# A hybrid decoder layer in one core: late tiles two abreast, the last gate pair swapped, stores and loads moved to GpSimd's queue, the scan tied behind the level

## The chip, the core and the metric

The kernel runs on one core of one Trainium2 chip. The core has five engines that run their own instruction streams in order: TensorE (PE, with the weight loads shown apart as PEld), VectorE (DVE), ScalarE (ACT), GpSimd (POOL) and SyncE (SP). A DMA is issued by one of the engines' queues and moves data between the chip's memory and the core's SBUF; matmuls write to PSUM. The metric is the device time of one execution in microseconds. Times are medians of several runs; durations of single instructions come from one profiled execution.

## The reference

One layer on a sequence of 1024 steps, 1024 wide, in float32. `h` is an RMS norm of `x`. One input projection of `h` gives the inputs of two branches and two gates. Branch A is an RWKV-7 time mix: 8 heads of 64, each a 64x64 state with a decay and a rank-one correction in every step. Branch B is S5, a diagonal complex state space with a GELU and a gated linear unit (GLU) behind it. Both are projected, gated and added, go through an output projection and a post norm, and are added to `x`. Then a gated MLP with a causal convolution of width 3 follows, with norms on both sides.

```python
h = rms_norm(x, norm_mix_pre[l])
proj = h @ w_in[l]
gates = jax.nn.sigmoid(proj[..., N_RWKV_COLS + S5_WIDTH:] + b_gate[l])
g_rwkv, g_s5 = jnp.split(gates, 2, axis=-1)
o_rwkv = rwkv7_branch(p_rwkv, ...) @ w_branch_rwkv[l]
o_s5 = s5_branch(u_s5, ...) @ w_branch_s5[l]
mixed = (g_rwkv * o_rwkv + g_s5 * o_s5) @ w_out[l]
x = x + rms_norm(mixed, norm_mix_post[l])
h = rms_norm(x, norm_ffn_pre[l])
f = conv_ffn(h, ffn_w_up[l], ffn_conv_w[l], ffn_conv_b[l], ffn_w_down[l])
x = x + rms_norm(f, norm_ffn_post[l])
```

## The kernel before

**Tiles.** Everything is held transposed: channels on the 128 partitions, time along the row, in two halves `th` of 512 steps. A product in float32 is made of three matmuls with reduced operands: each operand is split into a high part (a cast on ACT) and a low part (a subtraction on VectorE), and high x high, high x low and low x high are added up in PSUM. `mm3_steps` (L163) issues the three matmuls of each of the input blocks `k`; `load_w` (L145) loads a weight tile on SP's queue and splits it (L157 on ACT, L158 on VectorE). `split` and `split_half` (L226, L230) do it for activations. The two halves of `h` lie in the tile pools `hp[0]` and `hp[1]`, as pairs `hh0..7` and `hl0..7`, and those places are used again for later pairs.

**Order.** TensorE runs in the order in which the program is written (`manual_schedule`). The other engines' order is made by a scheduler that takes instructions by priority as its own model finds them ready; it is fixed before the run. The program text itself is woven from generators ("lanes") by `drive` (L186): a lane yields how long its matmuls take and how long to wait before its next piece, on a planner's clock `now`; in the gaps the `fill` list runs (`background`, L210), which holds the large projections. The constants `T_...` at L1905 to L1913 are such waiting times.

**Stages to about 960 us.** The norm and S5's inputs come first. Then the fill runs through the rest of the input projection (`mix_in`, L1009) and the 16 gate tiles (`gate_tiles`, L1030), of which the last two go as one pair through `inproj` (L915): both for `th` 0, then `merge_values`, then both for `th` 1. Their results go through the buffers `ev` (4 of them early, 3 later) to scratch tensors in memory: `RKV`, `TZ`, `TA`, `TG` (L999, L1006) and `GT` (L1035), with DMAs on SP.

Beside the fill the RWKV branch runs in four batches (2 groups of heads x 2 halves). `rwkv_front` (L642) loads `k`, `tz`, `ta`, `r` and later `v` (L659, SP) into the ring `ld` of 10 tiles, scans the decays (L674, VectorE), takes exponentials, makes products on GpSimd (L683, L684) and then the small matrices (L704, L706). `rwkv_inv` (L750) solves small triangular systems on VectorE (L763, L765), with GpSimd's DMAs before and after (L712, L756, L768, L775). `rwkv_level` (L777) transposes on VectorE (L787) and multiplies (L790, L792). `rwkv_chain` (L805) goes through 8 steps in series. `rwkv_out` (L866) normalizes and stores the branch's output `YR` (L911); the last batch keeps its output on the core, and its `bv` and `TG` loads (L878) go over GpSimd.

**The merge.** `merge` (L1159) forms the gated sum for `th` 0: eight gate tiles on branch A, S5's inputs loaded, put through GELU and split after the first of them, four GLU tiles (`glu_tile`, L1128) and eight gate tiles on branch B. `out_glu` (L1219) makes the output projection for `th` 0, with at most one GLU tile of `th` 1 after each of the tiles 3 to 7. `merge_s5` and `merge_rk` (L1228, L1246) form the sum for `th` 1, and `outproj(1)` (L1309) its output projection. `mid_norms` (L1313) is the post norm and the next norm; for `th` 0 it starts as soon as its sums `y0` are there, beside `merge_rk`. `first_units` (L1390) begins the MLP with the normalized `th` 0, which is split in the order 0, 4, 1, 5, 2, 6, 3, 7 and used in the order 0 to 7. The rest of the MLP (`fast_up`, `down`) isn't touched.

Of the kernel before, what the change touches and what calls it, by code (L numbers as in the profile page):

```python
# [72 lines left out]
class Kern:  # L73
# [89 lines left out]
    def mm3_steps(self, ps, w, wk, xh, xl):  # L163

        wh, wl = w
        n = len(xh)
        for k in range(n):
            j = wk + k
            self.open += (k == 0) - (k == n - 1)
# [3 lines left out]
            mm(ps, a, xh[k], start=k == 0, stop=False)  # L173
            mm(ps, a, xl[k], start=False, stop=False)  # L174
            mm(ps, b, xh[k], start=False, stop=k == n - 1)  # L175
            yield 0.68

# [464 lines left out]
    def rwkv_front(self, d, u):  # L642
# [14 lines left out]
        def ld(src):  # L657
            t = self.tg("ld", NLD)
            nc.sync.dma_start(t, src[:, o])  # L659
# [14 lines left out]
        V.tensor_tensor_scan(tz, self.cst("smask"), tz, 0.0, ALU.mult, ALU.add)  # L674
# [7 lines left out]
        for h, sl in enumerate(HS):  # L682
            G.tensor_tensor(ar1[h], c64(r)[sl], pe[sl, :, 1:65], ALU.mult)  # L683
            G.tensor_tensor(bk1[h], c64(tk)[sl], c64(tz)[sl], ALU.mult)  # L684
# [92 lines left out]
    def rwkv_level(self, d):  # L777
# [8 lines left out]
        for h, sl in enumerate(top):  # L786
            V.transpose(xz[sl].rearrange("p u c t -> p (u c) t"), gr[sl, :, :, h, sl].rearrange("p u c t -> p (u c) t"))  # L787
# [77 lines left out]

    def rwkv_out(self, d):  # L866
# [29 lines left out]
        yield 0, T_LN  # L896
        for u in range(2):
# [12 lines left out]
            else:  # L910
                nc.sync.dma_start(self.YR[p][:, o], y1)  # L911
# [3 lines left out]
    def inproj(self, *jobs, between=None):  # L915

        ws = [self.load_w(self.a["w_in"][mt]) for mt, _ in jobs]
        for th in range(2):
# [4 lines left out]
            if between and th == 0:  # L923
# [204 lines left out]
    def glu_tile(self, m, xs, t, y, to):  # L1128

        nc = self.nc  # L1130
        w = self.load_w(self.a["w_glu"][m])
        ps = self.gmp()
# [15 lines left out]
    def merge_values(self):  # L1148

        if self.outs < 2:  # L1150
            return
        self.br0 = []
        for k in range(4):
            y = self.tg("ld", NLD)
            self.nc.gpsimd.dma_start(y, self.YR[k][:, 0:512])
            self.br0.append(self.pair(0, k))
            self.split(*self.br0[k], y)

    def merge(self, mg):  # L1159
# [6 lines left out]
        br = self.br0  # L1166
        xs = []

        def inputs():
            for b in range(4):  # L1170
# [825 lines left out]
```

## Time and profile before

| | |
|---|---|
| median of 3 runs | 1628.59 us (1625.99 to 1630.82) |
| the profiled execution | 1626.5 us, its span 1624.7 us |
| mean granted TensorE clock | 0.967 |
| busy: TensorE, VectorE, ACT, GpSimd | 1505.0, 1157.2, 717.6, 175.9 us |

The span runs from the first instruction to the last. A busy digit of the page stands for a fortieth of the span, 40.6 us, in tenths. A granted clock of 0.5 means that matmuls take twice as long. A row of the timeline has the start, the duration, the engine, the line of the kernel, the operation and its tiles, and in brackets how long the engine stood idle before it and what ended that. A row of the groups has, behind the count, the busy time in us, the mean of one in ns, and the idle time before them with its releasers. A row of the waits has who waited for what, the us in total, how often, and the longest.

### The profile page before, as it was taken

How to read it: one execution, taken by the hardware profiler on the slowest of the kernel's cores; microseconds unless marked ns; L12 is line 12 of the kernel's file. 1: busy time of each engine (PE TensorE's matmuls, PEld its weight loads, DVE VectorE, ACT ScalarE, POOL GpSimd, SP SyncE). 2: the span in 40 equal slices, each digit the busy share in tenths (PEclk: the TensorE clock that was granted, in tenths of full speed). 3: DMA queues.
4: the chain of work that ended last, by engine and by line, in shares of the span. 5: the costliest groups of instructions: out<-in, count | busy, mean ns of one | idle time of the engine just before them, and what ended most of it. 6: DMA issues, size and time to landing. Idle time of an engine off the chain costs nothing. (4 is left out here: it accounts for less than half of the span.)

```text
span 1624.7 us, 23434 instructions
## 1 busy us (share of the span) xinstructions
PE 1505.0 (93%) x8644; PEld 1200.3 (74%) x8644; DVE 1157.2 (71%) x2103; ACT 717.6 (44%) x1173; POOL 175.9 (11%) x251
## 2 busy tenths in 40 slices
PE   5998998999989997899978999999999999999995
PEld 4887887787666774666756878788888888788784
DVE  7888774565534687575478479987777777788777
ACT  5445433232444344446633445544454444443451
POOL 0030003133012133211020000000000000000000
PEclk9999999999998997999988999999999999999997
DMA  5353344343341256535255363322222224862722
GB/s 190 110 158 124 97 130 143 117 130 116 90 145 67 76 179 175 142 106 163 84 187 190 107 193 130 137 71 91 78 78 91 91 79 160 293 227 96 234 85 104
DMA packets 116387, 213.72 MB, mean 132 GB/s; under 512 B 22272, under 2 KB 28416, under 8 KB 116272
## 3 DMA queue, kind: packets, MB, share of 16 engines
q1 hardware_dynamic: 102960, 175.78, 33.8%
q0 software_dynamic: 11152, 32.20, 6.7%
q10 hardware_dynamic: 2160, 4.24, 0.7%
q8 instruction: 68, 1.11, 0.3%
q14 instruction: 47, 0.39, 0.1%
HBM read 157.12 MB, written 52.95 MB: 129 GB/s over the span
## 5 line engine op out<-in xcount | busy, mean ns | idle before, releaser
L173 PE MATMUL gm<-hh,wh 128*128 128x512 f32 x688 | 298.5, 434 | 17.9 <-DVE ev L961 5.5
L174 PE MATMUL gm<-hl,wh 128*128 128x512 f32 x688 | 277.8, 404 | 3.3 <-DVE hl L1126 2.0
L175 PE MATMUL gm<-hh,wl 128*128 128x512 f32 x688 | 276.4, 402 | 0.0
L158 DVE TENSOR_TENSOR wl<-wf,wh 128x512 fp32r<-128x512 f32 x183 | 127.9, 700 | 115.1 <-ACT wh L157 113.4
L157 ACT CAST wh<-wf 128x512 fp32r<-128x512 f32 x183 | 113.3, 620 | 185.2 <-PE gm L174 94.0
L173 PEld LDWEIGHTS gm<-hh,wh 128*128 128x128 f32 x688 | 133.5, 194 | 54.6 <-ACT hh L1125 6.3
L174 PEld LDWEIGHTS gm<-hl,wh 128*128 128x128 f32 x688 | 134.0, 195 | 30.6 <-DVE hl L228 4.3
L175 PEld LDWEIGHTS gm<-hh,wl 128*128 128x128 f32 x688 | 133.6, 194 | 30.2 <-DVE wl L158 0.7
L1608 PE MATMUL d<-xl,wh 128*128 128x512 f32 x308 | 120.3, 391 | 3.1 <-DVE xl L228 3.1
L1607 PE MATMUL d<-xh,wh 128*128 128x512 f32 x308 | 120.2, 390 | 2.0 <-DVE zg L1463 2.0
L1609 PE MATMUL d<-xh,wl 128*128 128x512 f32 x308 | 119.9, 389 | 0.0
L1433 PE MATMUL rp<-t,h 128*128 128x512 f32 x216 | 84.4, 391 | 2.2 <-ACT p L1447 1.6
L1435 PE MATMUL rp<-t,l 128*128 128x512 f32 x216 | 84.2, 390 | 0.5 <-DVE l L228 0.5
L1434 PE MATMUL rp<-t,h 128*128 128x512 f32 x216 | 84.1, 389 | 0.0
L1608 PEld LDWEIGHTS d<-xl,wh 128*128 128x128 f32 x308 | 57.8, 188 | 16.7 <-DVE xl L228 4.8
L1607 PEld LDWEIGHTS d<-xh,wh 128*128 128x128 f32 x308 | 57.8, 188 | 14.4 <-DVE zg L1463 2.4
L1609 PEld LDWEIGHTS d<-xh,wl 128*128 128x128 f32 x308 | 57.8, 188 | 11.9
L227 ACT CAST h<-r 128x1024 fp32r<-128x1024 f32 x34 | 35.8, 1054 | 61.1 <-PE rp L1434 29.6
L228 DVE TENSOR_TENSOR l<-r,h 128x1024 fp32r<-128x1024 f32 x34 | 41.6, 1225 | 29.2 <-ACT h L227 27.7
L1454 DVE SCALAR_TENSOR_TENSOR y<-zv,vecs,y 128x1023 f32<-128x1023 f32 (+1 forms) x36 | 46.1, 1281 | 8.6 <-ACT y L1452 8.6
L1433 PEld LDWEIGHTS rp<-t,h 128*128 128x128 f32 x216 | 40.5, 188 | 11.8 <-ACT p L1447 2.4
L1447 ACT COPY p<-rp 128x512 f32<-128x512 f32 x54 | 31.1, 575 | 37.2 <-PE rp L1435 37.2
(446 smaller groups left out, 3400.4 us busy)
## 6 DMA issues: line engine op xcount, KB each, us to landing
wf<-in_w_in_dram SPq DMA_DIRECT2D x72, 256.0 KB, 3.0
r<-in_w_up_dram SPq DMA_DIRECT2D x36, 512.0 KB, 3.9
st<-in_w_down_dram SPq DMA_DIRECT2D x55, 256.0 KB, 4.3
st<-ACT SPq DMA_DIRECT2D x44, 256.0 KB, 4.7
wf<-in_w_up_dram SPq DMA_DIRECT2D x36, 256.0 KB, 2.9
ACT<-y POOLq DMA_DIRECT2D x18, 512.0 KB, 2.9
GT<-ev SPq DMA_DIRECT2D x32, 256.0 KB, 2.4
wf<-in_w_br_dram SPq DMA_DIRECT2D x32, 256.0 KB, 2.8
```

The costliest lines, as they stand in the source:

```text
L157: nc.scalar.copy(h[:, :n], f[:, :n])
L158: nc.vector.tensor_tensor(l[:, :n], f[:, :n], h[:, :n].bitcast(F32), ALU.subtract)
L173: mm(ps, a, xh[k], start=k == 0, stop=False)
L174: mm(ps, a, xl[k], start=False, stop=False)
L175: mm(ps, b, xh[k], start=False, stop=k == n - 1)
L1433: mm(ps, wh[:, c], xh, start=first and k == 0, stop=False, skip_group_check=True)
L1434: mm(ps, wh[:, c], xl, start=False, stop=False, skip_group_check=True)
L1435: mm(ps, wl[:, c], xh, start=False, stop=k == 3, skip_group_check=True)
L1454: V.scalar_tensor_tensor(y[:, lag:], z[:, 0:1024 - lag], self.vec(nme, i), y[:, lag:], ALU.mult, ALU.add)
L1607: mm(ps, wh[:, c], xh[:, x], start=start, stop=False, skip_group_check=True)
L1608: mm(ps, wh[:, c], xl[:, x], start=False, stop=False, skip_group_check=True)
L1609: mm(ps, wl[:, c], xh[:, x], start=False, stop=stop, skip_group_check=True)
```

## The change

It does nine things.

1. The stores of `RKV`, `TZ`, `TA`, `TG` and `GT`, the loads of `rwkv_front` and the loads and stores of `rwkv_out` are issued by GpSimd, not by SP.
2. The four products L683 and L684 of a front go from GpSimd to VectorE.
3. The scan L674 is ordered behind the transposes L787 of the level that was last written before it.
4. The pair of the last gate tiles runs `th` 1 first, then `th` 0. In between, `merge_values` now also loads and splits S5's inputs of `th` 0, into `hp[1]`; branch A's values go into `hp[1]` too, loaded straight into the tile of their low part, and the gate results of `merge` into `hp[0]`.
5. `out_glu` takes up to two GLU tiles after each of the tiles 4 to 7, and the GLU of `th` 1 fetches its factor `y` before its matmuls.
6. The last `rwkv_out` runs at a higher priority, and its planner wait is 11, not 16.
7. `mid_norms(0)` waits for the end of `merge_rk` and then 8, not 4; its wait before the sums is 24, not 55.
8. The first two tiles of `outproj(1)` run two abreast: inputs 0 to 5 of the first, 0 to 5 of the second, then 6 and 7 of both.
9. So does the first pair of `first_units`, in the order in which its inputs are split.

```diff
-    def mm3_steps(self, ps, w, wk, xh, xl):
+    def mm3_steps(self, ps, w, wk, xh, xl, ks=None, first=True, last=True):
...
+    def skewed(self, tiles, xs, ks, late):
+        xh, xl = [x[0] for x in xs], [x[1] for x in xs]
+        ps = [self.gmp() for _ in tiles]
+        ks = list(ks)
+        for p, (w, _) in zip(ps, tiles):
+            yield from self.mm3_steps(p, w, 0, xh, xl, ks[:-late], last=False)
+        for p, (w, use) in zip(ps, tiles):
+            yield from self.mm3_steps(p, w, 0, xh, xl, ks[-late:], first=False)
+            use(p)
...
-            nc.sync.dma_start(t, src[:, o])
+            G.dma_start(t, src[:, o])
...
-        V.tensor_tensor_scan(tz, self.cst("smask"), tz, 0.0, ALU.mult, ALU.add)
+        scan = V.tensor_tensor_scan(tz, self.cst("smask"), tz, 0.0, ALU.mult, ALU.add)
+        if self.levelled is not None:
+            self.tc.add_manual_dep(scan.ins, self.levelled.ins.name, ORDER)
...
-            G.tensor_tensor(ar1[h], c64(r)[sl], pe[sl, :, 1:65], ALU.mult)
-            G.tensor_tensor(bk1[h], c64(tk)[sl], c64(tz)[sl], ALU.mult)
+            V.tensor_tensor(ar1[h], c64(r)[sl], pe[sl, :, 1:65], ALU.mult)
+            V.tensor_tensor(bk1[h], c64(tk)[sl], c64(tz)[sl], ALU.mult)
...
+    def urgent(self, gen):
+        while True:
+            with self.tc.high_priority(HPN - HP2):
+                r = next(gen, None)
+            if r is None:
+                return
+            yield r
...
-                (G if final else nc.sync).dma_start(t, src)
+                G.dma_start(t, src)
...
-        yield 0, T_LN
+        yield 0, T_LF if final else T_LN
...
-                nc.sync.dma_start(self.YR[p][:, o], y1)
+                G.dma_start(self.YR[p][:, o], y1)
...
-        for th in range(2):
+        for th in (1, 0) if between else (0, 1):
...
-                    nc.sync.dma_start(dst[p][:, th * 512:th * 512 + 512], t)
+                    nc.gpsimd.dma_start(dst[p][:, th * 512:th * 512 + 512], t)
...
-                self.nc.sync.dma_start(self.RKV[mt][:, th * 512:th * 512 + 512], y)
+                self.nc.gpsimd.dma_start(self.RKV[mt][:, th * 512:th * 512 + 512], y)
...
-            self.nc.sync.dma_start(self.GT[m][:, th * 512:th * 512 + 512], t)
+            self.nc.gpsimd.dma_start(self.GT[m][:, th * 512:th * 512 + 512], t)
...
+        if ahead:
+            y = lambda v=y(): v
...
+        if not self.xs0:
+            for b in range(4):
+                y = self.s5_y(self.ev((128, 8, 64)), b, 0)
+                self.xs0.append(self.pair(1, 4 + b))
+                self.s5_split(*self.xs0[b], y)
...
-            y = self.tg("ld", NLD)
-            self.nc.gpsimd.dma_start(y, self.YR[k][:, 0:512])
-            self.br0.append(self.pair(0, k))
-            self.split(*self.br0[k], y)
+            hh, hl = self.pair(1, k)
+            self.nc.gpsimd.dma_start(hl.bitcast(F32), self.YR[k][:, 0:512])
+            self.br0.append((hh, hl))
+            self.split(hh, hl, hl.bitcast(F32))
...
-            if self.glu and m >= 3 and self.now >= self.glu_ready:
-                yield from self.glu.pop(0)
+            for _ in range(2):
+                if self.glu and m >= 4 and self.now >= self.glu_ready:
+                    yield from self.glu.pop(0)
...
     def outproj(self, th, mg, mx):
-        for m in range(NK):
+        yield from self.skewed([(self.load_w(self.a["w_out"][m]), lambda ps, m=m: self.outproj_end(th, m, mx, ps))
+                                for m in range(2)], mg, range(NK), 2)
+        for m in range(2, NK):
...
-            yield 0, lambda: self.y0 is not None
-            yield 0, T_RS
+            yield 0, lambda: self.merged
+            yield 0, T_PN
...
+    def up1_pair(self, i, th):
+        y = []
+        yield from self.skewed([(self.load_w(self.a["w_up"][j]), lambda ps, j=j: y.append(self.conv1(ps, j, th)))
+                                for j in (i, FT + i)], self.h[th], KORD, 2)
+        return y
...
-T_N0, T_RS, T_N1, T_N2, T_N4, T_N5, T_N3 = 2.5, 4.0, 2.2, 5.0, 1.6, 55.0, 2.0
+T_N0, T_RS, T_N1, T_N2, T_N4, T_N5, T_N3 = 2.5, 4.0, 2.2, 5.0, 1.6, 24.0, 2.0
+T_PN = 8.0
+KORD = (0, 4, 1, 5, 2, 6, 3, 7)
```

More of the change, by code (lines that the diff above doesn't have):

```diff
@@ L161, in load_w @@
         return wh, wl
-    def mm3_steps(self, ps, w, wk, xh, xl):
+    def mm3_steps(self, ps, w, wk, xh, xl, ks=None, first=True, last=True):
         wh, wl = w
-        n = len(xh)
-        for k in range(n):
+        ks = list(ks or range(len(xh)))
+        for k in ks:
             j = wk + k
-            self.open += (k == 0) - (k == n - 1)
+            a0, z0 = first and k == ks[0], last and k == ks[-1]
+            self.open += a0 - z0
             o = slice(j % 4 * 128, j % 4 * 128 + 128)
@@ L922, in inproj @@
                 use(th, ps)
-            if between and th == 0:
+            if between and th:
                 between()
@@ L1165, in merge @@
             self.merge_values()
[L1166 to L1170, printed above, removed]
-                y = self.s5_y(self.tg("ld", NLD, s8), b, 0)
-                xs.append(self.pair(1, 4 + b))
-                self.s5_split(*xs[b], y)
+        br, xs = self.br0, self.xs0
         yield 0
@@ L1177, in merge @@
             if i < NK:
-                first.append(self.hp[1].tile([128, 512], F32, tag=f"h{'lh'[i // 4]}{i % 4}", name=self.nm("hl"), bufs=1))
+                first.append(self.hp[0].tile([128, 512], F32, tag=f"h{'lh'[i // 4]}{i % 4}", name=self.nm("hl"), bufs=1))
                 yield from self.gate(0, i, 0, br[0:4], self.ev(), first[i])
-            if i == 0:
-                inputs()
             if MGAP <= i < MGAP + 4:
@@ L1335, in mid_norms @@
         self.h[th] = [None] * NK
-        for k in (0, 4, 1, 5, 2, 6, 3, 7):
+        for k in KORD:
             if th:
@@ L1898, in chain_lane @@
             out = self.rwkv_out(d)
-            r = next(out)
-            if i == 3:
-                yield r
-                yield from out
+            if i < 3:
+                r = next(out)
+            else:
+                yield from self.urgent(out)
 T_US, T_TAB0, T_TAB, T_TRIG, T_SCAN = 5.0, 18.0, 20.0, 12.0, 13.0
```

28 lines of the change are left out of this document (17 added, 11 removed).

## The prediction

> **What bounds the kernel now.** I read the page first, then every stretch in which TensorE stood idle, in order of time, then the granted clock behind each, and last the queues of VectorE and GpSimd at those places.
>
> ```profile
> span 1624.7 us, 23434 instructions
> PE 1505.0 (93%) x8644; PEld 1200.3 (74%) x8644; DVE 1157.2 (71%) x2103; ACT 717.6 (44%) x1173; POOL 175.9 (11%) x251
> PE   5998998999989997899978999999999999999995
> PEclk9999999999998997999988999999999999999997
> ```
>
> TensorE is the bound: 93% busy, and in most slices full. The slices that are not full lie at the start, at the very end, and at 7 to 9 of 10 between about 120 us and 960 us. From 960 us on nothing of the change acts. So its worth is read from the holes before 960 us. These are the larger ones: start, duration, instruction, and in brackets the idle time before it and its releaser.
>
> ```profile
> 280.89 0.79 PE L173 MATMUL gm<-hh,wh 128*128 128x512 f32 x1 [5.53 <-DVE ev L961]
> 489.41 0.31 PE L790 MATMUL chb<-ld,gr 32*32 32x32 f32 x2 [9.64 <-DVE ld L787]
> 613.43 0.50 PE L173 MATMUL gm<-hh,wh 128*128 128x512 f32 x1 [1.76 <-ACT hh L227]
> 634.79 0.79 PE L173 MATMUL gm<-hh,wh 128*128 128x512 f32 x1 [5.32 <-ACT hh L1125]
> 640.72 0.79 PE L174 MATMUL gm<-hl,wh 128*128 128x512 f32 x1 [1.71 <-DVE hl L1126]
> 817.03 0.50 PE L173 MATMUL gm<-e,wh 128*128 128x512 f32 x1 [1.26 <-ACT e L232]
> 821.14 0.80 PE L173 MATMUL gm<-e,wh 128*128 128x512 f32 x1 [2.31 <-ACT e L232]
> 849.16 0.49 PE L173 MATMUL mm<-hh,wh 128*128 128x512 f32 x1 [1.03 <-ACT hh L227]
> 853.02 0.79 PE L174 MATMUL mm<-hl,wh 128*128 128x512 f32 x1 [3.37 <-DVE hl L228]
> 884.97 0.80 PE L173 MATMUL mm<-t,wh 128*128 128x512 f32 x1 [4.10 <-ACT t L232]
> 888.88 0.79 PE L173 MATMUL mm<-t,wh 128*128 128x512 f32 x1 [1.56 <-ACT t L232]
> ```
>
> Each hole is paid twice, because the clock is low behind it. In the windows the fields are length, busy time of PE, PEld, DVE, ACT, POOL, then the granted clock, DMA share and GB/s.
>
> ```profile
> 280.80:287.80 7.00, 6.91 (x18) 5.41 (x19) 3.97 (x29) 1.75 (x3) 0.00 (x0) 0.55 0.41 145
> 489.40:498.40 9.00, 8.57 (x76) 5.75 (x77) 5.84 (x4) 3.96 (x8) 8.09 (x8) 0.50 0.02 6
> 616.00:622.00 6.00, 5.54 (x15) 4.17 (x16) 5.20 (x10) 2.75 (x5) 4.17 (x6) 0.53 0.85 256
> 634.70:646.70 12.00, 9.29 (x31) 6.01 (x31) 7.99 (x10) 6.09 (x9) 0.00 (x0) 0.55 0.47 123
> 821.00:827.00 6.00, 5.60 (x14) 4.09 (x14) 5.02 (x17) 0.71 (x2) 1.26 (x3) 0.55 0.45 136
> 852.80:857.80 5.00, 4.78 (x13) 3.69 (x14) 3.35 (x7) 1.10 (x3) 0.54 (x1) 0.57 0.98 369
> 884.80:896.80 12.00, 9.93 (x25) 6.83 (x26) 5.32 (x9) 3.73 (x7) 0.00 (x0) 0.59 0.32 103
> 934.00:946.00 12.00, 8.23 (x24) 6.14 (x24) 8.56 (x23) 3.63 (x7) 0.00 (x0) 0.72 0.43 153
> ```
>
> A hole is worth its idle time plus, behind it, PE busy time x (1 - clock). **280**: 5.5 + 6.91 x 0.45 = 8.6 us. **489**: 9.6 + 8.57 x 0.50 = 13.9. **613 to 641**: 1.8 + 5.3 + 1.7 + 5.54 x 0.47 + 9.29 x 0.45 = 15.6. **817 to 853**: 1.3 + 2.3 + 1.0 + 3.4 + 5.60 x 0.45 + 4.78 x 0.43 = 12.6. **885**: 4.1 + 1.6 + 9.93 x 0.41 = 9.7. **935**: 12 - 8.23 idle, plus 8.23 x 0.28 = 6.1. Together 66.5 us, 4% of the span: the most that the change can bring.
>
> The Trainium skill, "TensorE: Matmul & The Clock Gate", section "Why this matters for your kernels", warns only of idle gaps of more than about 3 us. The 0.55 at 821 stands behind gaps of at most 2.31 us, so here shorter ones cost clock too. By the rule the clock terms at 616, 821 and 934 would not hang on these gaps, and the forecast would be some 7 us higher, 1593 us.
>
> **The change part by part.** First, what two of the holes are made of on VectorE and GpSimd.
>
> ```profile
> 271.97 1.75 DVE L158 TENSOR_TENSOR wl<-wf,wh 128x512 fp32r<-128x512 f32 x1
> 276.66 1.85 DVE L714 SCALAR_TENSOR_TENSOR ld<-ld,vecs,ld 128x512 f32<-128x512 f32 x1 [2.34 <-POOL ar L683]
> 487.54 1.23 DVE L674 TENSOR_TENSOR_SCAN ld<-csts,ld 128x512 f32<-128x512 f32 x1 [7.87 <-DMA ld<-TZ]
> L714 DVE SCALAR_TENSOR_TENSOR ld<-ld,vecs,ld 128x512 f32<-128x512 f32 x8 | 11.4, 1424 | 7.5 <-POOL ar L683 7.2
> L683 POOL TENSOR_TENSOR ar<-ld,gr 64x512 f32<-64x512 f32 x16 | 22.3, 1394 | 14.3 <-DMA ld<-RKV 13.8
> L684 POOL TENSOR_TENSOR bk<-ld,ld 64x512 f32<-64x512 f32 x16 | 23.2, 1455 | 7.4 <-DVE ld L681 6.9
> L692 DVE SCALAR_TENSOR_TENSOR ar<-gr 64x512 f32<-64x512 f32 x16 | 10.9, 684 | 0.3
> L1280 DVE SCALAR_TENSOR_TENSOR mx<-mx,vecs,rp 128x512 f32<-128x512 f32 x16 | 11.4, 743 | 0.6 <-PE rp L272 0.6
> ```
>
> *Products of a front to VectorE* (L683, L684). 32 instructions leave GpSimd (45.5 us) and cost VectorE about 32 x 0.684 = 21.9 us by L692, which has their shape. Given back: L714 runs 1.424 us beside them against 0.743 us for the same shape in L1280, so 8 x 0.68 = 5.4 us, and its 7.2 us of waiting for L683. Net some 9 us on an engine that is 29% idle. What it buys is order: at 272 to 280 us the weight split L158 took 1.75 us and L714 waited and took 1.85 us while the eviction L961, for which TensorE waited, stood behind them. Without it that hole falls to about 1.5 us: **gain 7 of 8.6**.
>
> *Scan behind the level.* VectorE runs in order: the scan waited 7.87 us for its load, and the level's transposes (L787), next on the engine, came straight after it. Tied behind them, the scan no longer blocks; their own inputs were there long before, but their tile needs a slot of the ring `ld`, some of which come free only when the stores of the batch before land. So L790 starts between 481 and 485 us, not at 489.4, and the clock falls half as far: bounds 4 to 13.9, **gain 9**. Late next: the scans themselves, which TensorE wants some 18 us later.
>
> *Queues.* 80 stores (24 RKV, 24 of the low-rank downs, 32 gates), 40 loads of fronts, 12 loads and 6 stores of outputs go from SP to GpSimd.
>
> ```profile
> 840.47 3.71 POOL L1143 DMA_DIRECT2D t<-GT  x7
> 842.00:846.00 4.00, 4.00 (x20) 3.33 (x19) 3.92 (x7) 1.77 (x3) 2.18 (x5) 1.00 0.85 290
> L768 POOL DMA_DIRECT2D xd<-x x16 | 10.3, 671 | 90.6 <-DVE x L765 90.6
> ```
>
> An issue of this size costs GpSimd 3.71 / 7 = 0.53 us, so 138 x 0.53 = 73 us against 45.5 us taken away: 176 becomes some 204 us of 1625, no bound. On SP, weight loads no longer wait behind a store whose data isn't there; I take nothing for that, since weights end none of the holes above. The cost is head of line: GpSimd also runs in order, and it waits (L768 alone 90.6 us in 4 waits). Bounds 0 and the rival below; I take 3 us of new waits.
>
> The Trainium skill, "SBUF — State Buffer", section "Who interferes with whom", speaks against these moves: a DMA issued by GpSimd can be held up by VectorE in its two-port modes, one issued by SP never. Here seven issues kept 0.53 us each while VectorE was 3.92 of 4 us busy, so this trace does not show it.
>
> *Last gate pair swapped, S5 inputs early.* The pair now ends on the first half (th = 0), so the second half's tiles `hp[1]` are free while the pair's last two tiles run: 16 steps that the code counts at 0.68 us, 11 us.
>
> ```profile
> L1119 POOL DMA_DIRECT2D ld<-YU x4 | 3.7, 916 | 1.6 <-DVE wl L158 1.3 <-DVE gr L690 0.3
> ```
>
> In that time the four YR loads and the four S5 loads are issued (4 x 0.53 + 4 x 0.92 = 5.8 us), land, and are split; before, S5 was begun only after the first gate, and TensorE met it at 634.8. VectorE is full there with an inverse, so a part may stay: **gain 12 of 15.6**.
>
> *GLU tiles two per output tile, y fetched ahead; final output urgent and its transposes 5 us of planner time earlier; first post-norm only after the merge.* The first two holes of 817 to 853 are a GLU result used at once; then it is several tiles old. The last is a split queued on VectorE behind a post-norm add that waits for a residual load; that add now comes later. **Gain 9.5 of 12.6.**
>
> *Two tiles abreast at the start of `outproj(1)`.* Its inputs 6 and 7 are wanted 12 steps, not 6, after the start: 6 x 0.68 = 4.1 us later, against 4.1 + 1.6 us of idle. And the post-norm's 16 instructions of about 0.7 us no longer stand in the queue of the gates, which nearly fills VectorE alone:
>
> ```profile
> 862.00:880.00 18.00, 18.00 (x81) 14.91 (x80) 17.23 (x30) 8.15 (x14) 0.00 (x0) 1.00 0.51 168
> ```
>
> **Gain 8 of 9.7.** *The first unit in the order of its inputs, two abreast*: the norm now has about 40 us of planner time after the merge against some 45 us of output tiles, so its splits are still just in time: **gain 3 of 6.1**, and 3 us of new waits where the later norm's sums reach TensorE.
>
> Sum: 7 + 9 + 12 + 9.5 + 8 + 3 = 48.5, less 6 of new waits, 42.5 us. The profiled execution took 1626.5 us (1.8 outside its span), so 1584; the median of the runs is 2.1 above it, so **1586 us**.
>
> **Rivals.** *The holes only move.* VectorE takes 9 us more and is full beside the inverses; the shown releaser goes and the next one, 1 to 4 us behind, stays, and with it the clock. Half of the gain: 1607. For: many holes are under 3 us, and the batches of splits are dense. Against: at 280, 489 and 853 the blocked instruction had its inputs. *Nothing comes of it*: a planner order that shifts as a whole, with new holes for old ones: 1628. *GpSimd's queue blocks (slower).* GpSimd waited for the end of an inverse and for fronts:
>
> ```profile
> POOL xd L768 <- DVE x L765: 90.6, 4, 35.6
> POOL pt L678 <- ACT gr L676: 91.9, 5, 31.5
> ```
>
> If stores of projections stand behind such a wait, the three or four `ev` buffers and the PSUM banks fill within three to four tiles of 5.5 us, some 18 us, and TensorE stops until it ends: 35.6 - 18 and 31.5 - 18 are 31 us, and three or more such waits with the low clock behind them some 60 us. It decides from the point where these stops exceed the 42 us won: 1645 us. For: in-order issue, waits of that length. Against: stores and most of GpSimd's work both follow TensorE's fixed order. *Stretched issues*: GpSimd's work can be drawn out beside VectorE.
>
> ```profile
> L998 POOL TENSOR_SCALAR ev<-ev 128x512 f32<-128x512 f32 x8 | 16.3, 2043 | 61.7 <-DVE cb L537 50.0 <-ACT ev L996 11.7
> ```
>
> Were the 138 issues drawn out to these 2.04 us, GpSimd would spend 138 x 1.5 = 207 us more, and if TensorE met a tenth of it, 21 us, the time would be 1607. This is what the rule of the SBUF page in the Trainium skill would do here; against it stands the row at 840.
>
> **How the numbers follow.** Forecast (1560 to 1604) 0.58, holes that move 0.19, stretched issues 0.03, nothing 0.08, blocked queue 0.12. Faster by over 0.3% (about what a measurement here can tell from no change, 5 us) is the first three: 0.80; within 0.08, slower 0.12. The low end takes all 66.5 us, 1560, and a little for the small holes not counted; the high end takes the moved holes at their worst, 1622, and leaves out the last two cases.
>
> **What would show it.** Right: no wait of TensorE over 5 us between 250 and 960 us, L787 ahead of the scan, L714 near 0.74 us, granted clock near 1.00 around the level, the S5 inputs and the start of `outproj(1)`. Wrong: waits of the eviction L961 or L1034 for `ev` buffers, with GpSimd standing before L768 or L678; VectorE releasing the same places 1 to 4 us later; or the level still late because its tile has no slot.

## The result and the profile after

The changed kernel takes **1606.43 us** (median of 4 runs, 1602.80 to 1611.36) against 1628.30 us for the kernel before beside it: ratio 0.9867, 95% interval 0.9831 to 0.9904. A second measurement with five rounds gave 1605.81 us and 0.9847 (0.9826 to 0.9869). It is faster, by some 23 us; 1586 had been forecast, with a range up to 1622. The direction and the range held, the size of the gain was a little over half of the forecast.

The page of the changed kernel first: the span, the busy times, and two rows of the 40 slices.

```profile
span 1601.3 us, 23401 instructions
PE 1499.5 (94%) x8644; PEld 1200.9 (75%) x8644; DVE 1153.6 (72%) x2135; ACT 717.0 (45%) x1173; POOL 206.1 (13%) x357
PE   5998999999999998899999989999999999999995
PEclk9999999999999998999999989999999999999997
```

GpSimd (POOL) came out as worked out: 206.1 us busy against a forecast of 204. VectorE (DVE) did not: it was to take 9 us more net of the waits that go, and 16.5 us more in busy time alone (21.9 less 5.4), but it is busy for 3.6 us less than before (1157.2). Lines have moved by up to 28: L787 is L801 now, L790 L804, L714 L728, L683 and L684 are L697 and L698, L1374 is L1402, L998 is L1021, L1034 L1057.

TensorE's timeline in the changed kernel: the larger waits between 250 and 960 us that this text speaks of, each with start, duration and instruction, and with the wait and its releaser in brackets.

```profile
269.74 0.47 PE L174 MATMUL gm<-hh,wh 128*128 128x512 f32 x1 [1.46 <-ACT ld L694]
310.22 2.67 PE L718 MATMUL rp<-ar,bk 64*128 64x128 f32 x16 [3.70 <-DVE gr L720]
476.81 0.31 PE L804 MATMUL chb<-ld,gr 32*32 32x32 f32 x2 [2.92 <-DVE ld L801]
580.93 1.19 PE L680 MATMUL rp<-csts,gr 128*128 128x2 f32 x8 [2.92 <-ACT gr L675]
620.72 2.04 PE L718 MATMUL rp<-ar,bk 64*128 64x128 f32 x14 [3.28 <-DVE bk L698]
633.98 1.13 PE L718 MATMUL rp<-ar,bk 64*128 64x128 f32 x14 [1.82 <-DVE gr L720]
813.74 1.95 PE L924 MATMUL rp<-csts,yn 128*128 128x128 f32 x8 [3.04 <-DVE yn L918]
934.08 0.77 PE L174 MATMUL mm<-hh,wh 128*128 128x512 f32 x1 [4.99 <-DVE t L1402]
```

The holes of before at 613 to 641 us (5.32, 1.76, 1.71), 817 to 853 us and 885 us are gone, those at 280 and 489 us are down to 1.46 and 2.92. But four of the eight rows are new places: 620.72, 633.98, 813.74 and 934.08. The wait of 3.70 us at 310 us is none of these: it stood in the kernel before too (3.72 us at 317 us), as did the waits of 2.25 and 2.02 us at 660 and 670 us (2.25 and 2.10 there), and the prediction had left these out of its list. The clock behind three of the rows, in windows with the fields of before:

```profile
476.80:485.80 9.00, 8.56 (x76) 5.74 (x77) 6.11 (x8) 4.91 (x9) 2.64 (x5) 0.50 0.54 179
620.70:630.70 10.00, 9.59 (x55) 7.74 (x56) 6.50 (x10) 1.26 (x2) 3.79 (x7) 0.56 0.20 52
934.00:950.00 16.00, 15.92 (x56) 13.46 (x57) 4.76 (x12) 3.14 (x5) 1.09 (x2) 0.60 0.24 84
```

The hole of 2.92 us still has 8.56 x 0.50 = 4.3 us of lost clock behind it, and the one at 934 comes to 4.99 + 15.92 x 0.40 = 11.4 us (6.6 us in the second execution, by a clock of 0.90).

**Where the time went.** To set stages side by side though they begin at different times, I took windows of 5 us over each whole execution, counted busy time x granted clock as TensorE's work and the rest as lost, and cut the executions where the same work was done. The stages are named by where they lie in the kernel before. The changed kernel stands twice (its two profiles); the last column is the loss in the kernels below that undo the part meant for that stage.

| stage, us of before | before lost | changed lost | forecast gain | measured gain | with the part undone |
|---|---|---|---|---|---|
| 256 to 345 (products) | 13.6 | 8.0, 6.0 | 7 | 5.6, 7.6 | products_back 10.2 |
| 476 to 527 (level) | 15.4 | 8.1, 13.5 | 9 | 7.3, 1.9 | scan_free 18.3 |
| 582 to 690 (S5 inputs, last fronts) | 28.2 | 24.1, 25.3 | 12 | 4.1, 2.9 | swap_back 29.9, queues_back 20.4 |
| 746 to 912 (GLU, norm, two abreast) | 26.2 | 9.9, 13.7 | 17.5 | 16.3, 12.5 | tail_back 16.2, norm_early 18.7, skew_back 14.8 |
| 912 to 989 (first unit) | 6.9 | 14.2, 10.4 | 0 (3 less 3) | -7.3, -3.5 | unpaired 7.2 |
| all else up to 1587 | 46.2 | 51.8, 46.2 | -3 | -5.6, 0.0 | |

The stage of the level differs by 5.4 us between two executions of one kernel, so differences of a few us in this table aren't read; what it and the traces tell of single stages rests on one execution of each kernel, and on two of the changed one. Two rows fall far short of the forecast: the S5 stage and the first unit.

### The profile page after: what moved, and what is told of

The parts are those of the page before. It is cut to its first block, busy times and chain, and to the rows that moved or that the text cites. A ratio compares the mean times of both kernels' runs of the same rounds, so it can differ in the third digit from the quotient of the medians.

```text
span 1601.3 us, 23401 instructions
## 1 busy us (share of the span) xinstructions
PE 1499.5 (94%) x8644; PEld 1200.9 (75%) x8644; DVE 1153.6 (72%) x2135; ACT 717.0 (45%) x1173; POOL 206.1 (13%) x357
## 4 chain that ended last, share of the span: by engine, by line
PE 68%; DVE 14%; DMA 7%; issue 5%; ACT 4%; POOL 2%; SPq 0%; DVEq 0%; ACTq 0%; POOLq 0%
PE gm L174 9%; PE gm L175 7%; PE gm L176 7%; PE rp L1470 4%; PE rp L1472 4%; PE rp L1471 4%; DMA st<-in_w_down_dram 2%; PE mm L1471 2%; PE mm L1470 2%; PE mm L1472 2%; DVE wl L158 2%; PE d L1645 2%; PE d L1644 2%; PE d L1646 2%; PE mm L175 1%
## 5 line engine op out<-in xcount | busy, mean ns | idle before, releaser
L158 DVE TENSOR_TENSOR wl<-wf,wh 128x512 fp32r<-128x512 f32 x183 | 125.1, 686 | 106.2 <-ACT wh L157 101.3
L176 PEld LDWEIGHTS gm<-hh,wl 128*128 128x128 f32 x688 | 132.0, 192 | 29.9 <-DVE wl L158 0.7
L175 PEld LDWEIGHTS gm<-hl,wh 128*128 128x128 f32 x688 | 132.4, 192 | 25.3 <-DVE hl L240 2.7
L1422 POOL DMA_DIRECT2D ACT<-y x18 | 9.6, 535 | 342.7 <-DVE y L1421 322.9
```

The source lines that it names most:

```text
L158: nc.vector.tensor_tensor(l[:, :n], f[:, :n], h[:, :n].bitcast(F32), ALU.subtract)
L176: mm(ps, b, xh[k], start=False, stop=z0)
```

## The experiments

All kernels but the last two undo one part of the change and keep the rest. Each was timed in five rounds against the kernel before. The last column is (ratio - 0.9857) x 1629 us, 0.9857 being the mean of the two ratios of the changed kernel; it is good to some 5 us.

| kernel | median, us | ratio, 95% interval | against changed, us |
|---|---|---|---|
| after_again | 1605.81 | 0.9847 (0.9826 to 0.9869) | |
| products_back | 1612.74 | 0.9906 (0.9887 to 0.9925) | +8 |
| scan_free | 1613.39 | 0.9891 (0.9868 to 0.9915) | +6 |
| queues_back | 1600.88 | 0.9816 (0.9798 to 0.9834) | -7 |
| unpaired | 1598.43 | 0.9811 (0.9789 to 0.9834) | -7 |
| swap_back | 1607.32 | 0.9851 (0.9826 to 0.9875) | -1 |
| tail_back | 1612.72 | 0.9897 (0.9879 to 0.9914) | +7 |
| conv_first | 1604.66 | 0.9841 (0.9821 to 0.9860) | -3 |
| skew_back | 1610.94 | 0.9898 (0.9874 to 0.9922) | +7 |
| norm_early | 1608.20 | 0.9882 (0.9858 to 0.9906) | +4 |
| best1 | 1588.36 | 0.9755 (0.9734 to 0.9777) | -17 |
| best2 | 1585.13 | 0.9733 (0.9705 to 0.9760) | -20 |

**The changed kernel once more (after_again).**

> The changed kernel itself once more, as the measure for the runs beside it: 1603 to 1608, whatever the theory. Its profile tells how far a single stage differs between executions: the level's wait 2 to 6 us, the hole behind the first unit again 4 to 5 us.

1605.81 us. The level waited 2.41 us, the matmul behind the first unit 4.99 again.

**The products back on GpSimd (products_back).**

```
-            V.tensor_tensor(ar1[h], c64(r)[sl], pe[sl, :, 1:65], ALU.mult)
-            V.tensor_tensor(bk1[h], c64(tk)[sl], c64(tz)[sl], ALU.mult)
+            G.tensor_tensor(ar1[h], c64(r)[sl], pe[sl, :, 1:65], ALU.mult)
+            G.tensor_tensor(bk1[h], c64(tk)[sl], c64(tz)[sl], ALU.mult)
```

> The changed kernel with the 32 products of a front on GpSimd again (L697, L698), all else kept. Theory A, a trade: the products on VectorE won the hole at 280 us of the kernel before (5.5 idle + cold clock) and made the new ones at 620.7 and 634.0 us (3.28 idle behind L698 itself, 1.82 behind L720, with a clock of 0.87 there). Undone, the hole near 270 us is 4 to 6 us again, no wait of TensorE has L698 as releaser, and 610 to 640 us loses 5 us less: net within 3 us of the changed kernel's 1606. Rival: the products pay everywhere and the holes at 620 and 634 come from the gates that fill VectorE there: then they stay, released by another line, and the time is 1611 to 1614.

8 us slower: the rival's time, though not by its mechanism. Two things that theory A said did not come. The hole near 270 us is 1.93 us, not 4 to 6: with the products on GpSimd as in the kernel before, VectorE's eviction L984 (269.68 us) is not queued behind L728 (270.41) here, where in that kernel the eviction L961 (280.10) stood behind L714 (276.66). And the stage of 582 to 690 us is no better, 25.8 us lost by the same count against 24.1 and 25.3: L698 is no releaser any more, but a larger wait stands in its place. The largest differences of this trace lie at the level, 17.3 us lost against 8.1 and 13.5. From the timelines of this kernel, TensorE first:

```profile
270.63 0.47 PE L174 MATMUL gm<-hh,wh 128*128 128x512 f32 x1 [1.93 <-ACT ld L694]
497.13 0.64 PE L806 MATMUL chk<-gr,ld 32*32 32x32 f32 x16 [5.73 <-ACT gr L807]
619.55 0.80 PE L174 MATMUL gm<-hh,wh 128*128 128x512 f32 x1 [7.37 <-ACT ev L1057]
```

ScalarE, ahead of the second of these:

```profile
494.93 0.81 ACT L694 ACTIVATE ld<-ld,ka,ka_h 128x512 f32<-128x512 f32 x1 [5.09 <-POOL bk L698]
```

ScalarE waited 5.09 us for a product on GpSimd, and the copy L807, for which the level's matmuls waited 5.73 us, came behind that operation. For the third, VectorE some us earlier:

```profile
609.98 3.83 DVE L158 TENSOR_TENSOR wl<-wf,wh 128x512 fp32r<-128x512 f32 x1
614.87 2.01 DVE L1149 TENSOR_TENSOR hl<-ev,hh 128x512 fp32r<-128x512 f32 x1
```

GpSimd beside it:

```profile
610.72 2.53 POOL L698 TENSOR_TENSOR bk<-ld,ld 64x512 f32<-64x512 f32 x2
613.33 1.52 POOL L697 TENSOR_TENSOR ar<-ld,gr 64x512 f32<-64x512 f32 x1
```

While GpSimd multiplies, a weight split that takes 0.69 us elsewhere takes 3.83 us. The S5 split L1149 behind it is late, ScalarE's eviction L1057 waited 4.49 us for that split, and TensorE 7.37 us for the eviction. The groups of instructions by line tell what the products do to VectorE as a whole; count, then busy time and mean ns of one, then idle time before. The changed kernel:

```profile
L728 DVE SCALAR_TENSOR_TENSOR ld<-ld,vecs,ld 128x512 f32<-128x512 f32 x8 | 6.0, 747 | 0.1
L698 DVE TENSOR_TENSOR bk<-ld,ld 64x512 f32<-64x512 f32 x16 | 10.8, 683 | 0.1
L777 DVE TENSOR_TENSOR tm<-x,mt 128x120 f32<-128x120 f32 (+24 forms) x124 | 32.1, 259 | 4.5 <-DMA mt<-md 2.4
```

The same two with the products on GpSimd:

```profile
L728 DVE SCALAR_TENSOR_TENSOR ld<-ld,vecs,ld 128x512 f32<-128x512 f32 x8 | 8.5, 1067 | 6.2 <-POOL ar L697 6.2
L777 DVE TENSOR_TENSOR tm<-x,mt 128x120 f32<-128x120 f32 (+24 forms) x124 | 37.9, 306 | 4.8 <-DMA mt<-md 2.4
```

VectorE is busy for 1153.3 us in this kernel and 1153.6 us with the 32 products of 0.683 us on it: the 21.6 us that they take are given back in full by the operations that run beside GpSimd's products otherwise. The forecast had let them cost 9 us net.

**The scan untied (scan_free).**

```
-        if self.levelled is not None:
-            self.tc.add_manual_dep(scan.ins, self.levelled.ins.name, ORDER)
```

> The changed kernel without the tie of the scan to the level's transposes. Theory A: the level of the second batch waits for VectorE behind the scan's load again: wait at its first matmul (2.92 us in the changed kernel, 9.64 before) 7 to 10 us, time 1611 to 1613. Rival: what the tie saves is small, because the loads, now on GpSimd's queue, come early enough or the transposes wait for their slot of the ring anyway (they waited 1.74 us for a store of YR in the changed kernel): wait 3 to 4 us and time within 2 us of 1606.

6 us slower, wait 7.79 us: theory A, by the time and the wait. In its trace (lines stand two lower behind the edit: L799 and L802 are the changed kernel's L801 and L804, and the L695 that writes ar is its product L697):

```profile
475.71 1.22 DVE L686 TENSOR_TENSOR_SCAN ld<-csts,ld 128x512 f32<-128x512 f32 x1
481.95 0.68 DVE L695 TENSOR_TENSOR ar<-ld,gr 64x512 f32<-64x512 f32 x1 [5.01 <-DMA ld<-RKV]
482.56 1.43 DVE L799 STREAM_TRANSPOSE ld<-gr 32x512 f32<-32x512 f32 x2
```

The scan comes early, but it brings the product behind it forward too, and that waits 5.01 us for its load with the transposes queued behind. With the products on VectorE, the tie holds these back too. With the tie, what is left of the wait is the slot that the prediction named, seen in the changed kernel on GpSimd:

```profile
464.96 0.54 POOL L1058 DMA_DIRECT2D GT<-ev  x1 [8.60 <-ACT ev L1057]
465.50 0.54 POOL L901 DMA_DIRECT2D ld<-bv  x1
```

and on VectorE:

```profile
476.06 1.43 DVE L801 STREAM_TRANSPOSE ld<-gr 32x512 f32<-32x512 f32 x2 [1.74 <-DMA YR<-ld]
```

The output's loads stand behind a gate's store that waits 8.60 us for its eviction; so the output, its store and the slot come late, and L801 waits 1.74 us for that store.

**The queues back (queues_back).** L671, L901, L934, L1022, L1029 and L1058 issue on SP again.

```
-            G.dma_start(t, src[:, o])
+            nc.sync.dma_start(t, src[:, o])
...
-            self.nc.gpsimd.dma_start(self.GT[m][:, th * 512:th * 512 + 512], t)
+            self.nc.sync.dma_start(self.GT[m][:, th * 512:th * 512 + 512], t)
```

> The changed kernel with all 138 moved DMAs on SP's queue again. Theory A (as forecast): the queues are worth about nothing by themselves, 1606 within 4 us, GpSimd busy 73 to 76 us less. Rival 1: the stores on GpSimd cost waits (L668/L680 of a front at 580.9 us went from 1.52 to 2.92): 3 to 5 us faster without them, 1602. Rival 2: weight loads on SP had been late behind stores in the small holes: 4 to 8 us slower, 1610 to 1614, with waits for wf as releasers of L157's casts.

7 us faster: rival 1, a little more than it gave, and the opposite of rival 2. GpSimd is 74 us less busy (131.8), so an issue costs 0.54 us as forecast, and that time is not what hurts. What hurts is the order. GpSimd's timeline in the changed kernel:

```profile
565.99 0.56 POOL L1058 DMA_DIRECT2D GT<-ev  x1 [7.44 <-ACT ev L1057]
566.55 0.54 POOL L901 DMA_DIRECT2D ld<-bv  x1
568.67 0.54 POOL L671 DMA_DIRECT2D ld<-RKV  x1
```

ScalarE's in the same kernel:

```profile
575.24 0.72 ACT L675 ACTIVATE gr<-ld,vecs 128x512 f32<-128x512 f32 x1 [3.81 <-DMA ld<-RKV]
```

The same place with the queues back, in best1 (below), on SP's queue:

```profile
560.77 0.45 SPq L901 DMA_DIRECT2D ld<-bv  x1
562.68 0.43 SPq L671 DMA_DIRECT2D ld<-RKV  x1
567.87 0.32 SPq L1058 DMA_DIRECT2D GT<-ev  x1
```

and on ScalarE, with no wait ahead of it:

```profile
570.17 0.72 ACT L675 ACTIVATE gr<-ld,vecs 128x512 f32<-128x512 f32 x1
```

On GpSimd the loads of an output and of a front stand behind a store that waits 7.44 us for ScalarE; on SP they are issued ahead of that store. ScalarE's first operation of the front then waits 3.81 us for its load, and TensorE waits for the front (580.93 above; 2.92 us, against 1.02 in queues_back). Over the stage of 582 to 690 us the queues are worth 4 to 5 us (20.4 against 24.1 and 25.3 lost). The same count gives 18.0 and 19.7 us for best1 and best2, which have the queues back as well, and 23.6 or more for every kernel that has these loads on GpSimd. The profiled span of queues_back, 1600.6 us, is nevertheless that of the changed kernel, because its level lost 16.1 us in that execution. TensorE waits a second time there, 3.22 us at L806, and best1 and best2 show this too (3.44 and 2.08 us); whether the queues cause it was not tested.

**The first unit unpaired (unpaired), and its evictions ahead of the norm (conv_first).**

```
-            if i:
-                ga = yield from self.up1_steps(i, th)
-                va = yield from self.up1_steps(FT + i, th)
-            else:
-                ga, va = yield from self.up1_pair(i, th)
+            ga = yield from self.up1_steps(i, th)
+            va = yield from self.up1_steps(FT + i, th)
```

> The changed kernel with the first up-projection unit as before: its two tiles one after the other. Theory A: the new hole at 934 us (4.99 idle, then a clock of 0.83 over 40 us) is the pair's: its two tiles end together, and both evictions stand on VectorE behind the 16 operations of the later norm. Unpaired, the first tile is evicted before these, the hole at 934 goes, the waits for splits at its start go from 1.7 to about 4 us: net 4 to 8 us faster, 1598 to 1602. Rival: the hole is there because the norms come later relative to the output tiles (the wait for the merge): it stays at 3 to 5 us, and the time is 1606 to 1609.

```
-                        self.fill, self.fill_prio = [self.first_units(0)], 0
+                        self.fill, self.fill_prio = [self.first_units(0)], HP2 + HP
```

> The changed kernel with the evictions of the first units ranked above the later norm on VectorE and ScalarE (a priority of 300000 in place of 0), the pair kept. Theory A, the hole at 934 us is there because the pair's evictions stand behind the norm's 16 operations: it goes, and with it some 8 to 10 us, while the norm ends 6 us later, which may open 1 to 3 us at 971: 1597 to 1600. Rival: the hole is there because two tiles of the pair keep their PSUM banks until both end, whoever comes first on VectorE: it stays at 3 us or more, 1604 to 1608.

Unpaired is 7 us faster, as theory A had it: no hole is left at 934 us, and the splits at the unit's start are waited for 2.44 us. Ranking the evictions higher changes the time by no more than its error. That is the rival's time, but neither side's mechanism: the wait for L1402 does go, and one nearly as long opens elsewhere. The timeline of VectorE in the changed kernel:

```profile
910.16 1.41 DVE L1302 SCALAR_TENSOR_TENSOR mx<-mx,vecs,rp 128x512 f32<-128x512 f32 x2 [2.63 <-PE rp L284]
926.75 0.74 DVE L1402 SCALAR_TENSOR_TENSOR t<-mm,vecs,t 128x511 f32<-128x511 f32 x1
933.19 1.40 DVE L1402 SCALAR_TENSOR_TENSOR t<-mm,vecs,t 128x510 f32<-128x510 f32 x2
```

TensorE in unpaired, its longest wait at the start of the unit:

```profile
911.17 0.51 PE L174 MATMUL mm<-hh,wh 128*128 128x512 f32 x1 [2.44 <-ACT hh L239]
```

TensorE in conv_first:

```profile
937.40 1.87 PE L258 MATMUL rp<-ones,tm 128*128 128x1 f32 x8 [4.76 <-ACT tm L270]
```

The later norm, that of the second half (`mid_norms(1)`), occupies VectorE on and off from 910 to 926 us, and the unit's evictions come behind it. In the kernel before, the unit's first tile was evicted at 948 us and the norm began at 950. Two abreast, both tiles end when the norm is under way, so no PSUM buffer comes free, and when two more tiles have used the rest, TensorE stops until 934 us. With the evictions first, the norm's squares L270 come late instead, and the program's order has TensorE meet their sums (L258): 4.76 us. VectorE and ScalarE have both pieces of work to do in that time; finishing one tile earlier, as unpaired does, spreads them.

**The gate pair and the S5 inputs back (swap_back).** inproj, merge_values and merge as before.

```
-        for th in (1, 0) if between else (0, 1):
+        for th in range(2):
...
-            if between and th:
+            if between and th == 0:
...
+            if i == 0:
+                inputs()
```

> The changed kernel with the last gate pair in the old order, the S5 inputs again after the first gate and the outputs loaded into the ring ld (inproj, merge_values and merge as before). Theory A: this part won the S5 holes (5.32 and 1.71 us of wait for L1125/L1126, and 1.76 for the outputs' splits, with a clock near 0.54 behind them), and the holes at 617 to 634 us of the changed kernel are the front that now comes out late in their place: undone, 5 to 8 us slower than the changed kernel, 1611 to 1614. Rival: moving the products to VectorE alone freed GpSimd for the S5 loads and won these holes: then this part is worth nothing, within 3 us of it.

No difference in the time: the rival's number, not its mechanism. The old holes are back in its timeline of TensorE, though the products are on VectorE:

```profile
615.61 0.79 PE L175 MATMUL gm<-hl,wh 128*128 128x512 f32 x1 [1.81 <-DVE hl L240]
628.72 0.50 PE L174 MATMUL gm<-hh,wh 128*128 128x512 f32 x1 [1.46 <-ACT hh L1148]
632.63 0.74 PE L175 MATMUL gm<-hl,wh 128*128 128x512 f32 x1 [1.45 <-DVE hl L1149]
638.88 1.75 PE L718 MATMUL rp<-ar,bk 64*128 64x128 f32 x16 [0.78 <-DVE gr L720]
```

Two more, 1.90 and 2.62 us at 606 and 611 us, stand ahead of these; none is as long as the 5.32 us of before. Cut by work as above, the holes of the outputs' and S5 splits cost 15.5 us here and 3.8 and 2.0 us in the changed kernel's two executions: the swap does win the 12 us that were forecast. But the next piece, up to the matmuls L718 of the last front, costs 0.8 us here and 8.2 and 10.3 there. TensorE, no longer held up, arrives before VectorE has made the front (620.72, behind L698), and waits there.

**The GLU tiles and the last output back (tail_back), the norm early (norm_early), outproj(1) one after the other (skew_back).**

```
-            for _ in range(2):
-                if self.glu and m >= 4 and self.now >= self.glu_ready:
-                    yield from self.glu.pop(0)
+            if self.glu and m >= 3 and self.now >= self.glu_ready:
+                yield from self.glu.pop(0)
...
-        yield 0, T_LF if final else T_LN
+        yield 0, T_LN
```

tail_back also fetches the GLU's y late and leaves the last output without its priority.

> The changed kernel with the GLU tiles one per output tile from m = 3 and with their y fetched late, and the last output neither urgent nor with its transposes earlier. Theory A: undone, the waits for GLU splits at 817 to 821 us of the kernel before (1.26 and 2.31) are back, the hole at 813.7 us (3.04, L924) goes: 0 to 4 us slower than the changed kernel. Rival, the forecast's: this part and the later norm are worth 9.5 us, most of it here: 1613 or more.

```
-            yield 0, lambda: self.merged
-            yield 0, T_PN
+            yield 0, lambda: self.y0 is not None
+            yield 0, T_RS
```

norm_early also has T_N5 at 55 again.

> The changed kernel with the first post-norm gated as before (it starts when its factor is there, and its sums come 55 us of planner time later). Theory A: its 16 operations stand among the last gates' on VectorE again, the wait of 3.37 us for a split at 853 us of the kernel before is back and the splits for outproj(1) are late by as much: 4 to 8 us slower, 1610 to 1614; the hole behind the pair of the first unit (4.99) stays, as the later norm is its cause. Rival: the norm after the merge gives back at the first unit what it wins at the gates: the start of the first unit loses 2 to 3 us less, time within 3 us of 1606.

```
-        yield from self.skewed([(self.load_w(self.a["w_out"][m]), lambda ps, m=m: self.outproj_end(th, m, mx, ps))
-                                for m in range(2)], mg, range(NK), 2)
-        for m in range(2, NK):
+        for m in range(NK):
             yield from self.outproj_tile(th, m, mg, mx)
```

> The changed kernel with the tiles of outproj(1) one after the other from the start. Theory A (as forecast): the first two tiles abreast hide the wait for the last two splits of the merge; undone, waits of about 4 and 1.5 us with a clock near 0.6 behind them come back there (860 to 880 us): 7 to 9 us slower, 1613 to 1615. Rival: the post-norm, now after the merge, had freed VectorE there already: waits under 2 us, time within 3 us of 1606.

Slower by 7, 4 and 7 us, each good to some 5: tail_back is at its rival's time, the other two between both sides, and their traces decide. One row of TensorE's timeline from each, tail_back first:

```profile
811.54 0.79 PE L174 MATMUL gm<-e,wh 128*128 128x512 f32 x1 [2.31 <-ACT e L244]
```

norm_early:

```profile
869.22 0.80 PE L174 MATMUL mm<-t,wh 128*128 128x512 f32 x1 [1.71 <-ACT t L244]
```

skew_back:

```profile
861.83 0.50 PE L174 MATMUL mm<-t,wh 128*128 128x512 f32 x1 [1.25 <-ACT t L244]
```

tail_back brings both waits for GLU splits back whole (1.26 and 2.31 us) and the wait for the last output's split nearly so (2.89 us), and in return the wait of 3.04 us at L924 goes: the rival's time, with theory A's waits. The other two bring back a part each. With the norm early the splits for outproj(1) are late by 1.71 us though the tiles are abreast; with the tiles one after the other they are late by 1.25 us though the norm is late; before, both together made 4.10. For the norm theory A is half met: its stage lost more (18.7 against 9.9 and 13.7) and the splits for outproj(1) are late, but no wait like the 3.37 us of before at 853 us is back. For outproj(1) the waits are the rival's, under 2 us. The hole behind the first unit stayed at 4.99 us with the first norm early, so it doesn't hang on the place of the first half's norm.

**Two versions from these results (best1, best2).** best1 has both edits of unpaired and queues_back; best2 also has T_LF at 14.

> The changed kernel with both parts undone whose removal made it faster: the first unit unpaired and the 138 DMAs on SP's queue. Theory A, they are independent (8 and 5 us): 1593, ratio near 0.977. Rival: the 5 us of the queues, which the profiled executions did not show, are scatter of the runs: 1598, as unpaired alone.

> The kernel of best1 with the last output's transposes 3 us of planner time later (T_LF 14 in place of 11). Theory A: TensorE reaches them too early now (3.04 us of wait for yn L918, clock 0.91 behind it), and 3 us later the wait is gone: 3 to 4 us faster than best1, 1589 to 1590. Rival: the end of that chain, the output and the gates behind it, comes 3 us later, and the waits for splits after it grow by as much: same as best1.

best1 takes 1588.36 us, 17 us off the changed kernel: the two losses were real and add up, within the error (7 and 7 alone). best2 took 1585.13, and TensorE's wait at L924 is gone from its trace (3.04 us in best1); its interval overlaps that of best1, so only the wait is shown to go, not its price.

```profile
span 1586.5 us, 23422 instructions
PE 1496.4 (94%) x8644; PEld 1199.4 (76%) x8644; DVE 1154.2 (73%) x2135; ACT 716.5 (45%) x1173; POOL 131.3 (8%) x219
```

Both are faster than the kernel before (by 2.5 and 2.7%) and than the changed one.

## Why the prediction was right in direction and short in size

It said that TensorE's holes before 960 us are all there is to win, and that this is read hole by hole with its clock. That held: the holes named went or shrank, no wait of over 5 us is left between 250 and 960 us, and elsewhere (the table's last row) no more changed than differs between two executions. Step by step:

- *Products, gain 7 of 8.6*: right in size, while its cause is shown only in part. The stage gained 5.6 and 7.6 us, but with the products alone back on GpSimd it loses 10.2 us, not the 13.6 of before, and the eviction is not behind L728 again. So the order that this part was to buy came mostly without it, from what else had changed; no run tells from what. Undoing the part costs 8 us; by its trace some 3 of them lie in this stage and more at the level. The cost was off too, "Net some 9 us on an engine that is 29% idle": net nothing, since more had been stretched than L714 (747 ns now, as forecast). L158, L777 and L779 had been as well.
- *Scan behind the level, gain 9*: the order is as forecast (L801 ahead of the scan), the slot is what remains, as it had been named; the stage gained 7.3 and 1.9 us and undoing costs 6. It fell short because the wait of 2.4 to 2.9 us that is left has 9 to 10 us of clock at 0.50 behind it, as the wait of 9.64 us had (9.3 us, up to 498.7). That "the clock falls half as far" is the part that failed. The second execution lost more there because the clock was at 0.50 once more, from 493.5 to 503.7 us.
- *Queues, 3 us of new waits*: mis-sized, 7 us. The rival had stores of projections behind GpSimd's long waits. What came is the reverse: loads of fronts and outputs behind stores that wait 7 to 9 us for ScalarE. It stayed far from the 18 us that would have filled the buffers, so the rival's 1645 was not met.
- *Gate pair swapped, gain 12 of 15.6*: **this is the first term that failed.** The holes themselves gave 12 us, as forecast, but 7 to 9 us of them were lost within the next 20 us at the last front, L698, and undoing the part costs nothing. The text had said that "VectorE is full there with an inverse, so a part may stay"; it then priced the part by the hole and not by the engine. The sentence in the first rival, "the next one, 1 to 4 us behind, stays", is what happened (3.28 us).
- *GLU, output and norm, gain 9.5, and two abreast, gain 8*: right, somewhat short. The stage gained 16.3 and 12.5 of 17.5 us; the earlier transposes of the last output had a price that was not counted, the wait of 3.04 us at L924.
- *First unit, gain 3 of 6.1, less 3*: **the second term that failed**, by its sign. The price of two abreast was counted at the start of the pair alone, in splits that come in time. At its end both evictions stand behind the operations of the second half's norm, which the prediction had not looked at: some 7 us lost, by the time without the pair.

In the sum, by the table and the mean of its two executions: the S5 stage fell 8.5 us short (4 to 5 of it the queues'), the first unit 5.4, the level 4.4, the stage of GLU and norm 3.1 and the products 0.4, together 21.8 of the 42.5 us. Undone singly, the parts sum to 8 + 6 - 7 - 7 - 1 + 7 + 4 + 7 = 17 us against some 23 together; with some 5 us of error in each, that does not tell whether they simply add. At the S5 holes they do not: the piece that costs 15.5 us without the swap and 3.8 and 2.0 in the changed kernel costs 10.7 without the products, so both parts are needed there.

The time of the first rival, 1607, was met almost exactly, and that is luck: it isn't that half of every hole came back, but the stages of the products, the GLU, the norm and the tiles of outproj(1) gave nearly all that was asked, the swap next to nothing, and the queues and the first unit took. The rival of stretched issues had the same 1607, and it is out: an issue costs 0.54 us.

## What to carry to other kernels

Price a stall by the engine that feeds the next few steps, not by its own length: if VectorE is full across the stage, a hole that is closed opens again where its next result is wanted. Where two tiles are put abreast to wait less at the start, look at what their evictions meet when both end together. And on a queue that works in order, put loads that others wait for ahead of stores that wait themselves, or on another queue.

## What the runs showed of the hardware

VectorE's operations with two inputs are drawn out while GpSimd multiplies from SBUF: 3.83 us for a split of 0.69 us, and 1.067 against 0.747 us in the mean of L728. The sum is even here: 21.6 us of products moved to VectorE left its busy time unchanged (1153.6 us with them, 1153.3 without). The Trainium skill, "SBUF — State Buffer", section "Who interferes with whom", says that a VectorE instruction with two SBUF inputs contends with a GpSimd instruction that reads SBUF; the trace agrees, with these numbers. In the same section it warns of GpSimd's DMA issues beside VectorE in its two-port modes. Here the 138 issues took 0.54 us each in the mean, so their durations show nothing of it.

The granted clock: behind waits of 2.92 and 3.28 us it was 0.50 and 0.56 over 9 to 10 us, hardly better than the 0.50 behind 9.64 us of the kernel before. In narrow windows of these stretches it is 0.50 or 1.00, and a value between is a mean over both: behind the 3.04 us at 813.74 it is 0.50 from 813.8 to 817.2 us and 1.00 from there to 820.6. So what differs is how long it stays at 0.50, and that does not follow the length of the wait alone. Here are the 9 us behind the level's wait in best1, where that wait was 2.00 us, and in best2, where it was 1.32 us:

```profile
474.70:483.70 9.00, 6.72 (x82) 4.52 (x82) 3.10 (x4) 2.06 (x3) 0.57 (x1) 1.00 0.79 273
475.70:484.70 9.00, 8.46 (x76) 5.66 (x77) 2.49 (x3) 2.00 (x3) 0.00 (x0) 0.55 0.88 263
```

Behind the longer wait the clock stayed whole, behind the shorter one it fell. What decides between them no run here shows. Shortening a wait to about 3 us saved the wait at the level, but little of the clock.
